# Weighted sums of two heads in one product, a selection cut into steps, and held-back loads in a four-layer decoder trunk

## The chip, the core and the metric

The kernel runs on one core of one Trainium2 chip. The core has five engines, each with an instruction stream of its own: TensorE (PE in the profile; its weight loads are shown apart as PEld), VectorE (DVE), ScalarE (ACT), GpSimd (POOL) and SyncE (SP). They wait for one another through semaphores. Transfers between HBM and on-chip memory go through queues that SP, ACT and GpSimd issue to, and share 16 DMA engines. TensorE reads its operands from SBUF and accumulates in PSUM.

The metric is the device time of one execution in microseconds. The kernel before took 2635.22 us, the median of three runs (2634.94 to 2639.01).

## The reference

Four decoder layers over one sequence of 256 positions, width 2048, all in float32. Layer i uses mixer i mod 3: latent attention (layers 0 and 3), sparse attention with a learned selection (layer 1), sliding-window attention (layer 2).

```
mem_n = rmsnorm(mem)
for each layer:
    h = rmsnorm(x)
    streams, mq, gate = split(h @ w_in)
    self_out = mixer(streams)                  # 2048 wide
    mem_out  = softmax(mq . mk / 16) . mv      # 4 heads of 256; mk, mv = mem_n @ w_mem_kv
    y = concat(self_out, mem_out) * silu(gate) # 3072 wide
    x = x + y @ w_out
out = rmsnorm(x)
```

- Latent: 16 heads; a query of 1536 compressed values gives each head 128 plain and 64 rotary values (`w_uq`); keys and values come from 512 compressed values (`w_ukv`); one rotary key serves all heads.
- Sparse: 32 heads of 64 in 4 groups; 16 small index heads score every key, and each query keeps its 64 best ones. A relative-position bias is added.
- Sliding window: 32 heads of 64 in 4 groups, window 128, a learned sink for each head, the same bias table.

## The kernel before

**Products in two parts.** Every weight is split into a high part rounded to fp32r and the remainder (`parts_of`, `split`, lines 60 and 64: ACT makes `wh`, DVE makes `wl`), and so are the activations. A product is then a sum of products of parts. Weights come in tiles `wr` (`stage`, line 197, on SP's queue, five buffers), each split and used once. `rows_by` (lines 227 to 229) puts positions on the output's partitions, with up to 512 weight columns as the moving side: six products for each block of 128 rows, three for each half of the positions. `columns_by` (lines 246 and 250) puts 128 weight columns on the partitions and moves 512 and 256 positions.

**Stages.** First the memory stage (`memory`): for all four layers, memory keys (`acc_mk`) and values (`acc_mv`) are computed and stored to HBM through GpSimd's queue, 2 MB for each of eight steps. In the same stage come the constants, the rows of x, and eight copies (`table_copies`, line 133, 1.5 MB each) that repeat the bias table for 128 partitions in HBM: two copies in step 1, none at the last step, one in each of the others. Then come the layers. Each layer begins with `first()`: keys and values of the mixer, for layer 1 also `select()`, for layers 1 and 2 also the padded values `vz` (two GpSimd fills and splits). Then six parts follow, in the order 4, 0, 1, 2, 3, 5, where 4 and 5 are the two halves of the memory attention and 0 to 3 the groups of self heads. Each part projects its queries and its gate (`acc_g`), attends, and gives `y`; the output projection of the part before (`w_out`, `acc_wo`, line 832 for the residual) is traced behind it.

**Order of work.** The order on each engine comes from a scheduler that works from a simulated timeline and the tile pools' buffers, so work traced behind other work may run ahead of it. `keep_in_program_order` pins an instruction behind all that was traced before it on its engine. GpSimd's queue is in order too: the memory keys and values are loaded on it (`mvr` line 480, `mkr` line 483), as are the bias blocks `bm` (line 775).

**Self attention of layers 1 and 2** (`Grouped.attend`). For each of eight heads of a group: scores (`sp`), softmax, transposes of the weights to PSUM (`ptp`, line 427), a split into `pT` and `hl` (128 x 384, the three blocks of 128 that the causal order leaves), and the weighted sum `o` (line 811): for key half 0 three products of 256 columns, for key half 1 three of 128. The heads go in the order 0 to 7. `vz` holds a group's 64 value columns with 64 zero columns ahead and behind, so that an even head lands on partitions 64 below its odd neighbour and both accumulate in the same rows of `o`. After four heads `gated` multiplies by the gate.

**Selection** (`Grouped.select`, lines 738 to 764). For each half of the queries: 16 heads of two products (`isp`), a ReLU on ACT, a running weighted sum on DVE, then eight rounds of "eight largest" and "replace them" on DVE (lines 760 and 761).

**Rotary queries of layers 0 and 3** (`Latent.project`, lines 610 to 619). For each of four groups the 64 rotary columns of four heads, 256 in all, go through `rows_by` (`acc_qr`, 12 blocks of 128 rows), then through `rope` on DVE, a split, four transposes (`tr`, from `qrs`) and a copy to `qrT`.

Of the kernel before, what the change touches and what calls it, by code (L numbers as in the profile page):

```python
# [8 lines left out]
F32 = mybir.dt.float32  # L9
# [18 lines left out]
PQ, AUX, WR = 5, 3, 5  # L28
# [3 lines left out]
def kernel(ctx: ExitStack, tc: tile.TileContext, a: dict, out: bass.AP,  # L32
# [23 lines left out]
    def part_tile(dt=F32R):  # L56
        return wk.tile([P, 512], dt, name="hl", tag="hl", bufs=3)
# [76 lines left out]


# [69 lines left out]

    def parts_of(wr, c0, n):
        wh = wp.tile([P, 512], F32R, name="wh", tag="wh", bufs=3)
        wl = wp.tile([P, 512], F32R, name="wl", tag="wl", bufs=3)
        split(wh[:, :n], wl[:, :n], wr[:, c0:c0 + n])
        return wh, wl  # L210

    def rows_by(xt, kts, w, k0, cols, name, prepare=None):


        acc = [ps.tile([P, 512], F32, name=f"acc_{name}{t}", tag="acc", bufs=4) for t in range(2)]
        for s in range(0, kts, ST):
            m = min(ST, kts - s)
            wr, n = stage(w, k0 + s, m, cols)
            if prepare is not None and s % 4 == 0:
                prepare(s // 4)  # L220
            for k in range(m):
                wh, wl = parts_of(wr, k * n, n)
                q = xt[(s + k) // 4]
                for t in range(2):
                    xh, xl = (q[:, v, (s + k) % 4, t * P:(t + 1) * P] for v in range(2))
                    first, last = s + k == 0, s + k == kts - 1
                    nc.tensor.matmul(acc[t][:, :n], xh, wh[:, :n], start=first, stop=False)  # L227
                    nc.tensor.matmul(acc[t][:, :n], xh, wl[:, :n], start=False, stop=False)  # L228
                    nc.tensor.matmul(acc[t][:, :n], xl, wh[:, :n], start=False, stop=last)  # L229
        return acc  # L230

    def columns_by(xt, kts, w, k0, cols, name):

        acc = [ps.tile([P, 2, S], F32, name=f"acc_{name}{j}", tag="acc", bufs=4) for j in range(2)]
        for s in range(0, kts, 2 * ST):
            m = min(2 * ST, kts - s)
            wr, n = stage(w, k0 + s, m, cols)
            for k2 in range(0, m, 2):
                wh, wl = parts_of(wr, k2 * S, 2 * S)
                for k in range(2):  # L240
                    kt = s + k2 + k
                    q = xt[kt // 4]

                    for j in range(2):
                        o = k * S + j * P
                        nc.tensor.matmul(acc[j], wh[:, o:o + P], q[:, :, kt % 4, :],  # L246
                                         start=kt == 0, stop=False)
# [57 lines left out]
    def memory():  # L305
# [50 lines left out]
        copies = [(v, g) for v in range(2) for g in range(4)]  # L356
        for i in range(depth):
            w = a["w_mem_kv"][i]
            for p_ in range(2):
# [116 lines left out]
    def memory_project(nm, i, w, mq0, g0, part):  # L476
        kT, qT = [], []
        v = [act.tile([P, 2, 512], F32R, name="mvr", tag="aux", bufs=AUX) for z in range(2)]
        for z in range(2):
            nc.gpsimd.dma_start(v[z], mv[i][part][:, z])  # L480
        for h in range(2):
            k = act.tile([P, 2, 2, S], F32R, name="mkr", tag="pq", bufs=PQ)
            nc.gpsimd.dma_start(k, mkT[i][2 * part + h])
# [7 lines left out]
    def memory_attend(nm, kT, v, qT, gT):  # L491
        y = act.tile([P, 2, 4, S], F32R, name="y", tag="y", bufs=2)
        for h in range(2):
# [21 lines left out]
            pH, pL = (wk.tile([P, 512], F32R, name="pT", tag="pT", bufs=2) for z in range(2))  # L515
# [23 lines left out]
    class Latent:  # L539
# [6 lines left out]
        def first(self):  # L546
# [11 lines left out]
            for t in range(2):  # L558
# [6 lines left out]
                hl = wk.tile([P, 2, 2, A_ROPE], F32R, name="krh", tag="krh", bufs=1)  # L565
# [38 lines left out]

        def project(self, g):
# [4 lines left out]
            qr = act.tile([P, 4, S], F32R, name="qrT", tag="aux", bufs=AUX)  # L610
            v = act.tile([P, 2, 512], F32, name="va", tag="aux", bufs=AUX)
            acc = rows_by(self.cT[:3], 12, wq, 0, (g * 768, 4, 192, A_NOPE, A_ROPE), "qr")
            for t in range(2):
                rr = wk.tile([P, 4, A_ROPE], F32, name="qrr", tag="z", bufs=3)
                rope(rr, acc[t][:, :S].rearrange("p (h d) -> p h d", h=4), t, 4)
                rs = wk.tile([P, 4, 2, A_ROPE], F32R, name="qrs", tag="qrs", bufs=1)
                split(rs[:, :, 0, :], rs[:, :, 1, :], rr)
                transposed(lambda i0, i1: qr[:, i0:i1, t * P:(t + 1) * P],
                           [rs[:, h].rearrange("p a b -> p (a b)") for h in range(4)])
# [13 lines left out]
            return qn, qr, kn, v, gate(self.nm, self.w, self.g0 + g * 512)  # L633

        def attend(self, qn, qr, kn, v, gT):
            y = act.tile([P, 2, 4, S], F32R, name="y", tag="y", bufs=2)
            for h in range(4):
# [15 lines left out]
                pT = wk.tile([P, 512], F32, name="pT", tag="pT", bufs=2)  # L653
# [10 lines left out]
    class Grouped:  # L664
# [7 lines left out]
        def first(self):  # L672
# [10 lines left out]
            if self.sparse:  # L683
                self.select()
# [34 lines left out]
        def select(self):  # L719
# [17 lines left out]
            nc.vector.tensor_scalar(iw, iw, 0.25, None, op0=OP.mult)  # L737
            for b in range(2):
# [3 lines left out]
                for h in range(16):  # L742
# [9 lines left out]
                    else:  # L752
                        nc.vector.scalar_tensor_tensor(sco[1 - cur][:, :n], rl[:, :n], c,
                                                       sco[cur][:, :n], op0=OP.mult, op1=OP.add)
                        cur = 1 - cur
                nc.vector.tensor_add(sco[1 - cur][:, :n], sco[cur][:, :n], caus[:, S - n:])
                cur = 1 - cur
                for it in range(8):
# [3 lines left out]
                    cur = 1 - cur  # L762
                nc.vector.tensor_scalar(self.sel[:, b, :n], sco[cur][:, :n], -2e38, NEG,
                                        op0=OP.is_gt, op1=OP.mult)

# [13 lines left out]
        def attend(self, g, q, bm, gT):  # L779
            y = act.tile([P, 2, 4, S], F32R, name="y", tag="y", bufs=2)  # L780
            for h in range(8):
# [24 lines left out]
                c0 = (h // 2 % 2) * S  # L806
                v0 = g * P + (64 if h % 2 == 0 else 0)
                for t in range(2):
                    ks = slice(t * S, t * S + S - t * P)
                    for n_, (z, p_) in enumerate(((0, pH), (0, pL), (1, pH))):  # L810
                        nc.tensor.matmul(o[:, c0 + t * P:c0 + S], self.vz[z][:, t, v0:v0 + P], p_[:, ks],
                                         start=h % 2 == t == n_ == 0, stop=h % 2 == t == 1 and n_ == 2)
                if h % 4 == 3:
                    gated(y, o, gT, (h // 4) * 2)
# [4 lines left out]
    memory()  # L819

    for i in range(depth):
# [23 lines left out]
        for n_, part in enumerate(order):  # L845
            if part >= 4:
                y = memory_attend(*memory_project(nm, i, mixer.w, mixer.mq0, mixer.g0, part - 4))
# [91 lines left out]
```

## Time and profile before

| | |
|---|---|
| median of three runs | 2635.22 us (2634.94 to 2639.01) |
| profiled execution | 2636.8 us |
| its span, first to last instruction | 2634.7 us |
| TensorE busy, products | 2601.2 us, 14556 |
| VectorE busy | 1884.1 us |
| ScalarE busy | 1628.8 us |
| GpSimd busy | 57.3 us |
| mean granted TensorE clock | 0.997 |
| moved by DMA | 511.70 MB, 194 GB/s |

How to read the rows. A group of instructions is named by line, engine, operation and "output<-inputs"; behind the shape stands the count, then the busy time in us, the mean duration of one in ns, and the idle time of the engine just before them. Products overlap one another, so the pace of TensorE is read from the distance of their starts and not from their durations. A row of the waits gives who waited for whom, the total in us, how often, and the longest. A row of the timeline gives start, length, and in brackets the idle time before. A row of windows gives for each engine the busy time, and behind them the granted clock, the share of the DMA engines and GB/s. "SPq" is an engine's own instruction queue.

### The profile page before, as it was taken

The numbers are of one execution on the slowest core, as the hardware profiler recorded it, in microseconds if no ns is written. First come the engines' busy times: TensorE is split into PE (matmuls) and PEld (weight loads), VectorE is DVE, ScalarE is ACT, GpSimd is POOL, SyncE is SP. The second block draws the span as 40 slices with busy tenths as digits, with TensorE's granted clock in tenths as the row PEclk, the third lists the DMA queues.
The fourth block names the chain that finished last, engine by engine and source line by source line (L and its number), as shares of the span: only waits on it lengthen the run. The fifth ranks groups of instructions, "written<-read, shape, count | busy, mean of one in ns | idle before, by whom it ended". The sixth has DMA issues, their size and how long they took to land.

```text
span 2634.7 us, 42943 instructions
## 1 busy us (share of the span) xinstructions
PE 2601.2 (99%) x14556; PEld 2254.7 (86%) x14556; DVE 1884.1 (72%) x4171; ACT 1628.8 (62%) x3476; POOL 57.3 (2%) x101
## 2 busy tenths in 40 slices
PE   8999999999999999999999999999999999999998
PEld 7888888888888889888888888888888888888886
DVE  6566656677767685877777776777778767776767
ACT  6455556556656566666666666676666655665655
POOL 1000000000000000000000000000000000000000
PEclk9999999999999999999999999999999999999999
DMA  9889886666557665555555555555555666655764
GB/s 305 279 287 300 281 256 198 166 185 168 169 160 224 192 192 172 167 183 170 173 163 191 188 190 177 173 172 178 189 168 162 205 165 186 165 170 156 226 183 135
DMA packets 456924, 511.70 MB, mean 194 GB/s; under 512 B 69584, under 2 KB 352480, under 8 KB 455552
## 3 DMA queue, kind: packets, MB, share of 16 engines
q1 hardware_dynamic: 443328, 451.75, 56.5%
q0 software_dynamic: 13088, 56.16, 6.6%
q8 instruction: 114, 1.87, 0.3%
q14 instruction: 106, 0.87, 0.1%
q10 hardware_dynamic: 288, 1.05, 0.1%
HBM read 489.91 MB, written 31.56 MB: 198 GB/s over the span
## 4 chain that ended last, share of the span: by engine, by line
PE 97%; DMA 1%; DVE 1%; ACT 0%; issue 0%; SPq 0%; ACTq 0%
PE acc_g L246 14%; PE acc_g L250 7%; PE acc_wo L227 7%; PE acc_wo L228 7%; PE acc_wo L229 7%; PE acc_mq L246 5%; PE acc_mk L246 5%; PE acc_qn L246 3%; PE acc_cq L246 3%; PE acc_mq L250 2%; PE acc_mk L250 2%; PE acc_q L227 2%; PE acc_q L228 2%; PE acc_q L229 2%; PE acc_mv L227 2%; PE acc_mv L228 2%
## 5 line engine op out<-in xcount | busy, mean ns | idle before, releaser
L64 DVE TENSOR_TENSOR wl<-wr,wh 128x512 fp32r<-128x512 f32 (+2 forms) x1776 | 1173.8, 664 | 645.1 <-ACT wh L60 614.2
L60 ACT ACTIVATE wh<-wr 128x512 fp32r<-128x512 f32 (+2 forms) x1776 | 1079.0, 609 | 837.3 <-PE acc_g L246 183.7
L246 PE MATMUL acc_g<-xT,wh 128*128 128x512 f32 x1536 | 489.0, 397 | 0.6 <-DVE z L257 0.6
L250 PEld LDWEIGHTS acc_g<-xT,wl 128*128 128x128 f32 x1536 | 285.2, 188 | 60.7
L250 PE MATMUL acc_g<-xT,wl 128*128 128x256 f32 x1536 | 311.0, 280 | 0.0
L228 PE MATMUL acc_wo<-wl,y 128*128 128x512 f32 x768 | 302.6, 394 | 0.6 <-DVE wl L64 0.5
L229 PE MATMUL acc_wo<-wh,y 128*128 128x512 f32 x768 | 299.1, 390 | 0.0
L246 PEld LDWEIGHTS acc_g<-xT,wh 128*128 128x128 f32 x1536 | 238.1, 189 | 4.8 <-issue 1.1
L227 PE MATMUL acc_wo<-wh,y 128*128 128x512 f32 x768 | 240.4, 393 | 0.7 <-ACT wh L60 0.6
L228 PEld LDWEIGHTS acc_wo<-wl,y 128*128 128x128 f32 x768 | 144.3, 188 | 30.0 <-DVE wl L64 1.4
L229 PEld LDWEIGHTS acc_wo<-wh,y 128*128 128x128 f32 x768 | 144.2, 188 | 28.4
L227 PEld LDWEIGHTS acc_wo<-wh,y 128*128 128x128 f32 x768 | 141.3, 188 | 27.8 <-ACT wh L60 1.0
L246 PE MATMUL acc_mk<-mT,wh 128*128 128x512 f32 x512 | 161.9, 398 | 2.4 <-ACT wh L60 2.4
L246 PE MATMUL acc_mq<-xT,wh 128*128 128x512 f32 x512 | 161.7, 397 | 0.0
L832 DVE TENSOR_TENSOR x<-x,acc_wo 128x512 f32<-128x512 f32 x192 | 125.7, 683 | 7.1 <-PE acc_wo L229 6.8
L246 PE MATMUL acc_qn<-cT,wh 128*128 128x512 f32 x384 | 123.2, 399 | 0.0
L246 PE MATMUL acc_cq<-xT,wh 128*128 128x512 f32 x384 | 120.8, 396 | 0.0
L250 PEld LDWEIGHTS acc_mk<-mT,wl 128*128 128x128 f32 x512 | 96.7, 189 | 23.4 <-DVE wl L64 0.8
L250 PEld LDWEIGHTS acc_mq<-xT,wl 128*128 128x128 f32 x512 | 93.7, 188 | 20.0
L250 PE MATMUL acc_mq<-xT,wl 128*128 128x256 f32 x512 | 102.5, 281 | 0.0
L228 PE MATMUL acc_q<-wl,xT 128*128 128x512 f32 x256 | 102.4, 400 | 0.0
L250 PE MATMUL acc_mk<-mT,wl 128*128 128x256 f32 x512 | 101.7, 280 | 0.0
(280 smaller groups left out, 4438.0 us busy)
## 6 DMA issues: line engine op xcount, KB each, us to landing
wr<-in_w_out_dram SPq DMA_DIRECT2D x192, 512.0 KB, 3.7
wr<-in_w_in_a_dram SPq DMA_DIRECT2D x176, 512.0 KB, 4.1
wr<-in_w_mem_kv_dram SPq DMA_DIRECT2D x128, 512.0 KB, 5.6
wr<-in_w_in_b_dram SPq DMA_DIRECT2D x112, 512.0 KB, 3.5
wr<-in_w_in_c_dram SPq DMA_DIRECT2D x104, 512.0 KB, 3.5
wr<-in_w_uq_dram SPq DMA_DIRECT2D x288, 128.0 KB, 2.6
tab<-flat POOLq DMA_DIRECT2D x8, 1536.0 KB, 11.1
wr<-in_w_in_a_dram SPq DMA_DIRECT2D x32, 288.0 KB, 3.0
```

What stands on the lines that cost most here:

```text
L60: nc.scalar.activation(o, i, AF.Copy, scale=scale)
L64: nc.vector.tensor_sub(lo, src, f32(hi))
L227: nc.tensor.matmul(acc[t][:, :n], xh, wh[:, :n], start=first, stop=False)
L228: nc.tensor.matmul(acc[t][:, :n], xh, wl[:, :n], start=False, stop=False)
L229: nc.tensor.matmul(acc[t][:, :n], xl, wh[:, :n], start=False, stop=last)
L246: nc.tensor.matmul(acc[j], wh[:, o:o + P], q[:, :, kt % 4, :], start=kt == 0, stop=False)
L250: nc.tensor.matmul(acc[j][:, 0, :], wl[:, o:o + P], q[:, 0, kt % 4, :], start=False, stop=kt == kts - 1)
L832: nc.vector.tensor_add(xs, xs, acc[t])
```

## The change

Five edits.

1. *Rotary product for two groups.* `rotary(g)` runs in groups 0 and 2 alone, behind the values of the group: one `rows_by` over the eight heads of two groups (512 columns), then the rope for two groups and two halves of positions. The "aux" pool has 4 buffers instead of 3.
2. *Two heads' weighted sums in one product.* The heads go in the order 0, 2, 1, 3, 4, 6, 5, 7. Two heads that share the value columns (0 and 2, 1 and 3) put their split weights side by side in tiles of 3 x 2 x 128, and one product moves 512 columns for key half 0 and 256 for key half 1. The output `o` is thus ordered half of positions, pair, position; the product with the gate reads it in that order. The "pT" pool has 4 buffers of 768 instead of 2 of 512, "hl" 2 instead of 3.
3. *Selection step by step.* The loops of `select` become a generator, `selection`, which stops after each index head and after each round; `rows_by` and `columns_by` trace two steps of it for each weight tile, and the first `attend` of layer 1 traces what is left. The padded values follow the selection.
4. *Table copies held back.* The eight copies leave the memory stage. Each is traced behind the first quarter of an output projection: six in layer 0, two in layer 1. `not_before(col)` puts a GpSimd copy of one column of the new residual ahead of it, pinned, so that the transfer waits for it.
5. *First memory keys held back.* In part 4 of each layer a `not_before` on the mixer's key tile stands ahead of the loads of the values and keys, which are pinned too.

Beside these, the scratch space for the descriptors of GpSimd's transfers is set to 8192 bytes for each partition, and the small rotary-key tile shares a buffer with `qrs`.

```diff
-PQ, AUX, WR = 5, 3, 5
+PQ, AUX, WR, PT = 5, 4, 5, 4
...
+    def not_before(col):
+        tc.keep_in_program_order(nc.gpsimd.tensor_copy(small("tick", 1), col))
...
+    steps = []
+    def other_work():
+        for _ in range(2):
+            if steps and next(steps[0], None) is None:
+                steps.pop()
...
             wr, n = stage(w, k0 + s, m, cols)
+            other_work()
...
-                for c in copies[:2 if step == 1 else 1]:
-                    table_copies(*c)
-                copies = copies[2 if step == 1 else 1:]
...
-    def memory_project(nm, i, w, mq0, g0, part):
+    def memory_project(nm, i, w, mq0, g0, part, behind):
         kT, qT = [], []
+        if part == 0:
+            not_before(behind)
...
+        pin = tc.keep_in_program_order if part == 0 else lambda inst: inst
         for z in range(2):
-            nc.gpsimd.dma_start(v[z], mv[i][part][:, z])
+            pin(nc.gpsimd.dma_start(v[z], mv[i][part][:, z]))
...
+        def rotary(self, g):
+            self.qr = [act.tile([P, 4, S], F32R, name="qrT", tag="aux", bufs=AUX) for z in range(2)]
+            acc = rows_by(self.cT[:3], 12, a["w_uq"][self.j], 0, (g * 768, 8, 192, A_NOPE, A_ROPE), "qr")
+            for t in range(2):
+                for z in range(2):
+                    rr = wk.tile([P, 4, A_ROPE], F32, name="qrr", tag="z", bufs=3)
+                    rope(rr, acc[t][:, z * S:(z + 1) * S].rearrange("p (h d) -> p h d", h=4), t, 4)
+                    rs = wk.tile([P, 4, 2, A_ROPE], F32R, name="qrs", tag="qrs", bufs=1)
+                    split(rs[:, :, 0, :], rs[:, :, 1, :], rr)
+                    transposed(lambda i0, i1: self.qr[z][:, i0:i1, t * P:(t + 1) * P],
+                               [rs[:, h].rearrange("p a b -> p (a b)") for h in range(4)])
...
-            return qn, qr, kn, v, gate(self.nm, self.w, self.g0 + g * 512)
+            if g % 2 == 0:
+                self.rotary(g)
+            return qn, self.qr[g % 2], kn, v, gate(self.nm, self.w, self.g0 + g * 512)
...
             if self.sparse:
-                self.select()
+                steps.append(self.select())
+            else:
+                self.spaced_values()
...
         def attend(self, g, q, bm, gT):
+            while steps:
+                other_work()
...
-            for h in range(8):
+            for h in (0, 2, 1, 3, 4, 6, 5, 7):
...
-                pH, pL = wk.tile([P, 512], F32R, name="pT", tag="pT", bufs=2), part_tile()
-                split(pH[:, :3 * P], pL[:, :3 * P], tp[:, :3 * P])
-                if h % 4 == 0:
+                half, odd = h // 2 % 2, h % 2
+                if half == 0:
+                    pHL = [wk.tile([P, 3, 2, P], F32R, name="pT2", tag="pT", bufs=PT) for z in range(2)]
+                split(pHL[0][:, :, half, :], pHL[1][:, :, half, :],
+                      tp[:, :3 * P].rearrange("p (i c) -> p i c", i=3))
+                if half == 0:
+                    continue
+                if not odd:
                     o = misc("o")
...
                 for t in range(2):
-                    ks = slice(t * S, t * S + S - t * P)
-                    for n_, (z, p_) in enumerate(((0, pH), (0, pL), (1, pH))):
-                        nc.tensor.matmul(o[:, c0 + t * P:c0 + S], self.vz[z][:, t, v0:v0 + P], p_[:, ks],
-                                         start=h % 2 == t == n_ == 0, stop=h % 2 == t == 1 and n_ == 2)
+                    for n_, (z, p_) in enumerate(((0, 0), (0, 1), (1, 0))):
+                        nc.tensor.matmul(o[:, t * S:], self.vz[z][:, t, v0:v0 + P],
+                                         pHL[p_][:, 2 * t:2 + t].rearrange("p i h c -> p (i h c)"),
+                                         start=odd == t == n_ == 0, stop=odd == t == 1 and n_ == 2)
...
+                if c == 0 and copies:
+                    not_before(xs[:, :1])
+                    table_copies(*copies.pop(0))
...
-    nc = _bacc.Bacc("TRN2", target_bir_lowering=False, num_devices=1)
+    nc = _bacc.Bacc("TRN2", target_bir_lowering=False, num_devices=1,
+                     dynamic_dma_scratch_size=8192)
```

More of the change, by code (lines that the diff above doesn't have):

```diff
@@ L514, in memory_attend @@
             tp = weights_T(es, [(0, 0), (1, 0), (0, 1), (1, 1)])
[L515 removed]
+            pH, pL = (wk.tile([P, 768], F32R, name="pT", tag="pT", bufs=PT)[:, :512] for z in range(2))
             split(pH, pL, tp)
@@ L564, in first @@
                 rope(kr, raw[:, None, :A_ROPE], t, 1)
-                hl = wk.tile([P, 2, 2, A_ROPE], F32R, name="krh", tag="krh", bufs=1)
+                hl = wk.tile([P, 4, 2, A_ROPE], F32R, name="krh", tag="qrs", bufs=1)[:, :2]
                 for d in range(2):
@@ L737, in select, with selection @@
             nc.vector.tensor_scalar(iw, iw, 0.25, None, op0=OP.mult)
+            return self.selection(iqT, ikd, iw)
+        def selection(self, iqT, ikd, iw):
             for b in range(2):
@@ L819 @@
     memory()
+    copies = [(v, g) for v in range(2) for g in range(4)]
     for i in range(depth):
@@ L846 @@
             if part >= 4:
-                y = memory_attend(*memory_project(nm, i, mixer.w, mixer.mq0, mixer.g0, part - 4))
+                y = memory_attend(*memory_project(nm, i, mixer.w, mixer.mq0, mixer.g0, part - 4,
+                                                  f32(mixer.k[:, 0] if kind else mixer.kr)[:, 0, :1]))
             else:
```

33 lines of the change are left out of this document (16 added, 17 removed).

## The prediction

> **What bounds the kernel.** I read the page first, then who waited for whom on TensorE, then the timeline of TensorE in steady stretches and around its gaps, then GpSimd's timeline at those gaps. The page:
>
> ```profile
> span 2634.7 us, 42943 instructions
> ...
> PE 2601.2 (99%) x14556; PEld 2254.7 (86%) x14556; DVE 1884.1 (72%) x4171; ACT 1628.8 (62%) x3476; POOL 57.3 (2%) x101
> ...
> GB/s 305 279 287 300 281 256 198 166 185 168 169 160 224 192 192 172 167 183 170 173 163 191 188 190 177 173 172 178 189 168 162 205 165 186 165 170 156 226 183 135
> ...
> PE 97%; DMA 1%; DVE 1%; ACT 0%; issue 0%; SPq 0%; ACTq 0%
> ```
>
> TensorE is busy 99% of the span and is 97% of the chain that ended last. Two things alone can move the time: fewer or denser products, and the few gaps. The first six slices (0 to 395 us, the memory stage) move 256 to 305 GB/s, the later ones mostly 160 to 190. The gaps, from the waits of TensorE:
>
> ```profile
> PE acc_mv L227 <- ACT wh L60: 10.0, 2, 8.7
> PE acc_kvb L227 <- ACT wh L60: 3.1, 1, 3.1
> PE acc_mk L246 <- ACT wh L60: 2.4, 1, 2.4
> PE o L811 <- ACT pT L60: 1.7, 3, 0.6
> PE ptp L427 <- ACT e L60: 1.4, 3, 0.5
> ```
>
> The 8.7 us is the start, which the change leaves alone. So 1.3 + 3.1 + 2.4 = 6.8 us are waits for weight parts and 1.7 + 1.4 = 3.1 us waits around the weighted sums of layers 1 and 2.
>
> **Rotary product for two groups.** It replaces 576 products of 256 columns (3 x 192) by 288 of 512: the order of the changed program has 192 + 96 of these. The columns stay the same, so only what a product costs beside its columns can be saved. The pace, first and last row of a steady run of each width:
>
> ```profile
> L228 PE MATMUL acc_qr<-wl,cT 128*128 128x256 f32 x192 | 52.0, 290 | 0.0
> L229 PE MATMUL acc_qr<-wh,cT 128*128 128x256 f32 x192 | 50.6, 283 | 0.0
> L227 PE MATMUL acc_qr<-wh,cT 128*128 128x256 f32 x192 | 40.3, 286 | 0.0
> ...
> 519.56 0.40 PE L227 MATMUL acc_qr<-wh,cT 128*128 128x256 f32 x2
> 525.31 0.40 PE L227 MATMUL acc_qr<-wh,cT 128*128 128x256 f32 x2
> ...
> 2608.04 0.62 PE L227 MATMUL acc_wo<-wh,y 128*128 128x512 f32 x2
> 2609.40 1.07 PE L227 MATMUL acc_wo<-wh,y 128*128 128x512 f32 x4
> ```
>
> From 519.56 to 525.31 start 48 products (eight blocks of six): 0.120 us each. From 2608.04 to 2609.40 start six: 0.227 us each. Saved: 576 x 0.120 - 288 x 0.227 = 69.1 - 65.4 = 3.7 us, all on the path. The durations of 283 to 290 ns are no pace, since products overlap.
>
> [...]
>
> The weight loads shrink from 96 transfers of 128 KB to 48 of 256 KB on SP's queue, and 96 pairs of half-width weight splits become 48 full ones on ACT and DVE. Both engines are at 62% and 72%, so that is worth nothing. The rope and the transposes keep their count but move into the gate product, where ACT and DVE run the same kind of load; the transposes stand there with 22 to 24 products between them, as they did among acc_qn, where TensorE shows no wait for them. Zero; at worst 0.5 us for each of 16, the size of the waits above, 8 us.
>
> **Two heads' sums in one product.** 384 products (192 of 256 columns, 192 of 128) become 96 of 512 and 96 of 256. One head now:
>
> ```profile
> L811 PE MATMUL o<-pT,vz 128*128 128x256 f32 x128 | 35.3, 284 | 1.7 <-ACT pT L60 1.7
> L811 PE MATMUL o<-pT,vz 128*128 128x128 f32 x128 | 28.5, 248 | 0.0
> ...
> 1196.09 0.28 PE L811 MATMUL o<-pT,vz 128*128 128x256 f32 x1
> ...
> 1196.61 0.28 PE L811 MATMUL o<-pT,vz 128*128 128x128 f32 x1
> 1196.72 0.68 PE L227 MATMUL acc_q<-wh,xT 128*128 128x512 f32 x2
> 1197.24 0.40 PE L228 MATMUL acc_q<-wl,xT 128*128 128x512 f32 x1
> ```
>
> Six products take 1196.09 to 1196.72 = 0.63 us, and the two wide ones behind them 0.52 instead of 2 x 0.227: 0.065 us more, lost behind the 128-column product. 64 heads x 0.695 = 44.5 us. After: 32 pairs x (3 x 0.227 + 3 x 0.120) = 33.3 us, with no 128-column product left in it. Saved: 11.2 us. [...]
>
> The waits around the sums (3.1 us): each stood where weights' transposes, sums and scores of neighbouring heads met with no weight product between. In the order of the changed program none of the sums follows such a transpose directly. I take all 3 us as gone; between 0 and 3.1. Next late is the softmax chain of two heads instead of one, with 10 to 40 weight products as cover; without it a wait is 0.6 us again. The four other buffers (PT, AUX, hl, big) cost no instruction; hl falls from 3 to 2 but loses its 64 uses in the sums. I put 1 us against it.
>
> **Copies and first keys held back.** GpSimd's queue ahead of the three gaps, then TensorE:
>
> ```profile
> 107.69 1.06 POOL L133 DMA_DIRECT2D tab<-flat  x2
> ...
> 289.66 0.53 POOL L133 DMA_DIRECT2D tab<-flat  x1
> ...
> 379.88 1.08 POOL L480 DMA_DIRECT2D mvr<-mv  x2
> 380.93 0.56 POOL L483 DMA_DIRECT2D mkr<-mkT  x1
> ...
> L133 POOL DMA_DIRECT2D tab<-flat x8: 529/530/547, 52.3 to 336.0; - x8
> ...
> wr<-in_w_mem_kv_dram SPq DMA_DIRECT2D x128, 512.0 KB, 5.6
> ```
>
> ```profile
> 126.38 0.73 PE L246 MATMUL acc_mk<-mT,wh 128*128 128x512 f32 x2 [2.44 <-ACT wh L60]
> ...
> 131.06 0.62 PE L246 MATMUL acc_mk<-mT,wh 128*128 128x512 f32 x2
> ...
> 131.76 0.63 PE L246 MATMUL acc_mk<-mT,wh 128*128 128x512 f32 x2
> ...
> 293.57 0.73 PE L227 MATMUL acc_mv<-wh,mT 128*128 128x512 f32 x2 [1.26 <-ACT wh L60]
> ...
> 391.92 0.53 PE L227 MATMUL acc_kvb<-wh,xT 128*128 128x288 f32 x2 [3.11 <-ACT wh L60]
> ...
> 396.96 0.43 PE L227 MATMUL acc_kvb<-wh,xT 128*128 128x288 f32 x2
> ...
> 397.75 0.42 PE L227 MATMUL acc_kvb<-wh,xT 128*128 128x288 f32 x2
> ```
>
> Behind the gap at 126.38 a step of two wide and two narrow products takes (131.06 - 126.38) / 4 = 1.17 us instead of 0.70, so 1.9 us are lost beside the 2.4. Behind that at 391.92 it is (396.96 - 391.92) / 4 = 1.26 instead of 0.79: 1.9 beside 3.1. The three waits with both tails are 6.8 + 3.8 = 10.6 us. I take 9 as gone, since the stores of memory keys and values stay in the stage; bounds 0 and 10.6.
>
> What it costs: 12 one-column copies on GpSimd (2% busy), and behind each of them the queue. Behind a residual column wait one table copy, later a bias load or a key load of part 5, none due for some 20 us; behind the key column wait four loads of 512 KB, wanted after two acc_mq products (128 x 2 products, over 40 us). The copies now run beside the output projection, at 160 to 190 GB/s instead of 280. Six of the eight ran singly in the busier stage, and only the one at 289.66 stands near a wait (1.3 us at 293.57). I take 1 us for all; at worst each stalls like the double one, 8 x 4.3 = 34 us.
>
> **Selection step by step.** The counts stay: 64 products, the sums, 16 rounds of maximum and replacement.
>
> ```profile
> L760 DVE MAX8 m<-sco 128x8 f32<-128x256 f32 x8 | 3.4, 422 | 0.0
> L761 DVE MATCH_REPLACE8 sco<-m,sco 128x256 f32<-128x256 f32 x8 | 3.3, 410 | 0.0
> ...
> 1040.00:1090.00 50.00, 50.00 (x323) 46.10 (x321) 35.20 (x87) 31.96 (x76) 1.06 (x1) 1.00 0.61 183
> 1090.00:1140.00 50.00, 50.00 (x284) 43.50 (x283) 45.05 (x112) 31.96 (x71) 2.12 (x3) 1.00 0.53 165
> ```
>
> TensorE (second number) has no gap there now, so nothing can be gained. The new order puts the last score products later, with about 120 gate products and 56 of the output projection before the first weights' transpose, over 30 us of cover for 8 x 0.83 = 6.7 us on a DVE at 45 of 50 us. If DVE falls behind, up to 6.7 us of it shows. I take 1 us.
>
> **Sum.** -3.7 - 11.2 - 3 - 9 + 1 + 1 + 1 = -23.9 us. The profiled execution took 2636.8 us (span 2634.7), so 2612.9; the median of the runs is 1.6 us lower, 2611.3.
>
> **Rivals.**
> 1. The weight waits stay, because the stage's own loads and stores make them: for it, the weights alone are 512 KB for every twelve products of 0.227 us, 192 of the stage's 280 GB/s, and stores of keys and values come on top; against it, a copy or key load stands 4 to 19 us ahead of each. Without the 9 us: 2620.
> 2. The products cost by their columns alone, 0.227 us for each 512, and what looks like a price of the narrow ones is spent again behind the wide ones: both parts save nothing, 2611.3 + 14.9 = 2626. The rows 0.120 and 0.227 speak against it. [...]
> 3. The held-back copies starve the output projection's weights, in layers 0 and 1 (slower). At 4.3 us each: 2611.3 + 34 - 1 = 2645. It decides from (23.9 + 1) / 8 = 3.1 us for each copy. The double copy did cost that; single copies in a busier stage did not.
> 4. The change does not do what it says: the waits only move, to the pair of heads (3 us), the transposes among the gates (8 us), the late selection (6.7 us) and one copy (4.3 us): 2611.3 + 22 = 2633.
>
> **Numbers.** Forecast 0.64, rival 1 0.18, rival 2 0.06, rival 3 0.06, rival 4 0.06. A change under 0.2% (5.3 us) is about what a measurement of this kernel can't tell from none. Faster 0.64 + 0.18 + 0.06 = 0.88, same 0.06, slower 0.06. Low end: 14.9 + 10.6 + 3.1 saved, nothing lost, and 0.065 us at some 100 further changes from one kind of product to another that fall away where sums are merged: 35 us, 2600, and 1 us for rounding. High end: rival 2, 2626. Rivals 3 and 4 and the tails of the others stay outside.
>
> **What would show it.** acc_qr with 288 products of 512 columns 0.227 us apart; o with 96 of 512 and 96 of 256, none of 128; TensorE's busy time down by some 15 us; no wait of acc_mk, acc_kvb above 1 us, and the first six slices near 230 GB/s. Wrong if TensorE waits for wh at acc_wo in layers 0 and 1, for e or pT at ptp and o, for qrs at tr, or if six sums take over 1.1 us.

## The result and the profile after

The changed kernel takes 2607.73 us, the median of four runs (2605.6 to 2610.79), against 2636.04 us of the kernel before in the same session (2634.94 to 2639.01). The ratio is 0.9893, with a 95% interval of 0.9878 to 0.9908: 28 us faster, between 24 and 32. The forecast was 2611. The profiled execution took 2605.6 us, its span is 2603.8 us.

The page of the changed kernel: span, busy times of the engines, GB/s in forty slices.

```profile
span 2603.8 us, 41703 instructions
...
PE 2579.8 (99%) x14076; PEld 2220.4 (85%) x14076; DVE 1875.0 (72%) x4123; ACT 1617.9 (62%) x3428; POOL 61.9 (2%) x113
...
GB/s 289 248 259 252 256 211 235 186 170 190 191 204 217 198 214 215 168 195 182 200 166 196 171 220 170 177 170 186 194 156 150 234 182 169 170 167 182 211 178 129
```

TensorE is busy 21.4 us less (2601.2 to 2579.8) where the prediction looked for "some 15", and the span is 30.9 us shorter. So about 9.5 us came from gaps. Some 3.8 us of the busy time aren't fewer products either: they are the two stretches at a lower clock behind the waits of acc_mk and acc_kvb (granted clock 0.59 and 0.57), which are gone too (the last section shows them). Here is what is left of the gaps, in the waits of TensorE (who waited for whom, total, times, longest):

```profile
PE acc_mv L240 <- ACT wh L60: 9.4, 4, 8.5
PE o L847 <- DVE pT L64: 0.3, 1, 0.3
```

Beside the start (8.5 us) there remain 1.2 us. The waits of acc_kvb and acc_mk are gone, and with them that of `ptp`; of `o` 0.3 us is left. Where the span became shorter can be read from acc_cq, the first product behind the mixer's keys in layers 0 and 3. Its first and last start, before and after:

```profile
L246 PE MATMUL acc_cq<-xT,wh x384: 387/395/475, 404.9 to 2118.3; 128*128 128x512 f32 x192
```

```profile
L260 PE MATMUL acc_cq<-xT,wh x384: 387/395/478, 394.3 to 2088.2; 128*128 128x512 f32 x192
```

The memory stage with the first keys is 10.6 us shorter in these two profiles, the stretch from there to the last acc_cq of layer 3 (1713.4 to 1693.9 us) 19.5, and the rest 0.8. The two merged products, in the groups by shape (`acc_qr` has two more groups of 96 like the one shown):

```profile
L242 PE MATMUL acc_qr<-wh,cT 128*128 128x512 f32 x96 | 37.4, 389 | 0.0
...
L847 PE MATMUL o<-pT,vz 128*128 128x512 f32 x96 | 32.6, 400 | 0.3 <-DVE pT L64 0.3
...
L847 PE MATMUL o<-pT,vz 128*128 128x256 f32 x96 | 16.7, 282 | 0.0
```

Their pace, from the timeline of TensorE (start, length):

```profile
542.02 0.62 PE L240 MATMUL acc_qr<-wh,cT 128*128 128x512 f32 x2
543.38 0.62 PE L240 MATMUL acc_qr<-wh,cT 128*128 128x512 f32 x2
...
1189.51 1.23 PE L847 MATMUL o<-pT,vz 128*128 128x512 f32 x6
1190.58 0.64 PE L240 MATMUL acc_q<-wh,xT 128*128 128x512 f32 x2
```

Six rotary products take 1.36 us, 0.227 each. The six of a pair of heads take 1.07 us, where 3 x 0.227 + 3 x 0.120 = 1.04 were forecast.

### The profile page after: what moved, and what is told of

Same layout as the page of the kernel before. It is cut to its first block, busy times and chain, and to the rows that moved or that the text cites. A ratio compares the mean times of both kernels' runs of the same rounds, so it can differ in the third digit from the quotient of the medians.

```text
span 2603.8 us, 41703 instructions
## 1 busy us (share of the span) xinstructions
PE 2579.8 (99%) x14076; PEld 2220.4 (85%) x14076; DVE 1875.0 (72%) x4123; ACT 1617.9 (62%) x3428; POOL 61.9 (2%) x113
## 4 chain that ended last, share of the span: by engine, by line
PE 98%; DMA 1%; DVE 1%; ACT 0%; issue 0%; SPq 0%; ACTq 0%
PE acc_g L260 14%; PE acc_g L264 7%; PE acc_wo L240 7%; PE acc_wo L241 7%; PE acc_wo L242 7%; PE acc_mq L260 5%; PE acc_mk L260 4%; PE acc_cq L260 3%; PE acc_qn L260 3%; PE acc_mq L264 2%; PE acc_q L241 2%; PE acc_q L240 2%; PE acc_q L242 2%; PE acc_mk L264 2%; PE acc_mv L240 2%; PE acc_mv L241 2%
## 5 line engine op out<-in xcount | busy, mean ns | idle before, releaser
L241 PEld LDWEIGHTS acc_wo<-wl,y 128*128 128x128 f32 x768 | 144.3, 188 | 28.3 <-DVE wl L64 0.6
```

## The experiments

Twelve kernels ran in three sessions. The kernel before had a median of 2633.84, 2636.92 and 2635.78 us in them, and every ratio is against the runs of its own session. Differences are told as differences of these ratios, times 2636 us.

| kernel | median us | ratio to before (95%) |
|---|---|---|
| before + rotary pair | 2631.65 | 0.9993 (0.9984 to 1.0003) |
| before + paired sums | 2617.2 | 0.9938 (0.9923 to 0.9952) |
| before + copies held back | 2632.2 | 0.9995 (0.9985 to 1.0004) |
| before + keys held back | 2647.17 | 1.0052 (1.0037 to 1.0067) |
| before + selection in steps | 2637.63 | 1.0004 (0.9995 to 1.0014) |
| before + keys + selection in steps | 2632.9 | 0.9986 (0.9976 to 0.9996) |
| changed, selection in one piece | 2624.73 | 0.9955 (0.9940 to 0.9969) |
| changed, keys not held back | 2613.13 | 0.9911 (0.9896 to 0.9925) |
| changed, copies not held back | 2611.46 | 0.9905 (0.9890 to 0.9919) |
| changed, each copy twice at once | 2627.62 | 0.9965 (0.9953 to 0.9977) |
| changed, each copy twice, apart | 2607.6 | 0.9893 (0.9878 to 0.9907) |
| changed, two loads earlier | 2604.14 | 0.9881 (0.9866 to 0.9895) |

### The rotary product alone

```diff
-            acc = rows_by(self.cT[:3], 12, wq, 0, (g * 768, 4, 192, A_NOPE, A_ROPE), "qr")
+            if g % 2 == 0:
+                self.rotary(g)     # (g * 768, 8, 192, A_NOPE, A_ROPE)
```

> The kernel before with the rotary product for two groups alone (aux 4, the smaller scratch space). Theory (a product has a price beside its columns): 288 products of acc_qr at 0.227 us instead of 576 at 0.120, so -3.7 us, and no wait for qrs among the gate products. Rival 2 (columns alone): 0 us. A rival from the order of work (the rope and its transposes come late among the gates): up to +8 us. The three weight waits of the memory stage and of acc_kvb stay as before under all of them, 6.8 us of waits in all.

Measured 0.9993: 1.8 us, between 4.2 gained and 0.8 lost. The time alone doesn't tell it from nothing. Its page shows TensorE busy 4.0 us less, and no wait for `qrs` appeared:

```profile
PE 2597.2 (99%) x14268; PEld 2239.3 (85%) x14268; DVE 1876.8 (71%) x4123; ACT 1625.2 (62%) x3428; POOL 57.3 (2%) x101
```

By the starts of acc_cq in that trace (404.9 to 2116.4 us, span 2631.6) the stretch with layer 0 is 1.9 us shorter and the one with the rest of layer 3 1.2, together 3.1.

### The paired sums alone

```diff
-            for h in range(8):
+            for h in (0, 2, 1, 3, 4, 6, 5, 7):
...
-                        nc.tensor.matmul(o[:, c0 + t * P:c0 + S], self.vz[z][:, t, v0:v0 + P], p_[:, ks],
+                        nc.tensor.matmul(o[:, t * S:], self.vz[z][:, t, v0:v0 + P],
+                                         pHL[p_][:, 2 * t:2 + t].rearrange("p i h c -> p (i h c)"),
```

> The kernel before with the two heads' sums in one product alone (head order, pT 4, hl 2, the smaller scratch space). Theory: -11.2 us from the products and the loss behind the 128-column ones, and -3 to -4 from the six waits around the sums, together about -15 us. Rival 2 (columns alone): -3 to -4 us, from the waits only. A rival in which the waits only move to the pair: -11 us, with waits of o and ptp of 3 us still there.

Measured 0.9938: 16 us, between 13 and 20, more than half of the whole change. Rival 2 (columns alone count) falls. TensorE's busy time from its page, and the waits of layers 1 and 2 that it still has:

```profile
PE 2585.2 (99%) x14364; PEld 2236.8 (86%) x14364; DVE 1882.3 (72%) x4171; ACT 1622.4 (62%) x3476; POOL 57.4 (2%) x101
```

```profile
PE o L814 <- DVE pT L64: 0.3, 1, 0.3
PE acc_wo L228 <- DVE wl L64: 0.2, 1, 0.2
```

Busy time fell by 16.0 us, where the forecast had 11.2. Beside the waits of `o` and `ptp`, three small ones in layers 1 and 2 shrank with them that the forecast had not counted. These are they, in the waits of the kernel before between 1200 and 2000 us:

```profile
PE acc_g L246 <- DVE z L257: 0.6, 3, 0.2
PE acc_wo L227 <- ACT wh L60: 0.6, 1, 0.6
PE acc_wo L228 <- DVE wl L64: 0.5, 1, 0.5
```

With the 1.7 and 1.4 us of `o` and `ptp` that is 4.8 us, of which 0.5 is left, so 4.3 us of waits went. Not all of the 16.0 belongs to the sums, though. Of the 20.5 us by which the profiled span fell, 2.2 lie ahead of acc_cq, in the memory stage, which this edit doesn't touch:

```profile
L246 PE MATMUL acc_cq<-xT,wh x384: 387/395/476, 402.7 to 2097.8; 128*128 128x512 f32 x192
```

There the wait of acc_mk was 1.4 us instead of 2.4 in this execution. The waits ahead of acc_cq add up to 15.5 us in both kernels, so the 2.2 us were busy time; that they are the stretch at a lower clock behind acc_mk (1.9 us in the kernel before) is an estimate. The stretch from acc_cq to the last acc_cq fell by 18.3 us (1713.4 to 1695.1): that is the sums' part, 4.3 us of waits and about 14 of busy time.

### The copies alone, the keys alone

Two kernels. The first takes the copies out of the memory stage and puts each behind a quarter of an output projection:

```diff
+                if c == 0 and copies:
+                    not_before(xs[:, :1])
+                    table_copies(*copies.pop(0))
```

> The kernel before with the eight table copies held back alone. Theory (the copies made the waits of the memory stage): the 2.4 us wait of acc_mk and its slow tail go, and part of the 1.3 us wait of acc_mv; -4.5 to -5.5 us; the wait of acc_kvb (3.1 us) stays, since the first keys are not held back. Rival 1 (the stage's own loads and stores make them): 0 us. Rival 3 (the copies starve the output projection): waits of acc_wo for wh appear, up to +34 us.

The second holds back the first memory keys and values:

```diff
+        if part == 0:
+            not_before(behind)
...
-            nc.gpsimd.dma_start(v[z], mv[i][part][:, z])
+            pin(nc.gpsimd.dma_start(v[z], mv[i][part][:, z]))
```

> The kernel before with the first memory values and keys of each layer held back alone. Theory: the 3.1 us wait of acc_kvb and its 1.9 us tail go, -5.0 us, and no new wait at acc_cq, where the four loads then run; the wait of acc_mk (2.4 us) stays. Rival 1 (the narrow blocks of 288 columns make the wait themselves): 0 us, the wait stays. Rival (the loads hit the next product instead): the wait moves to acc_kvb or acc_cq, between -3 and 0 us.

The copies gave 0.9995, which is not told from nothing and misses the 4.5 us or more of the theory; the keys made the kernel slower, 1.0052, by 13.7 us. No theory had that. The waits of TensorE in the two kernels, the copies' first:

```profile
PE acc_kvb L232 <- ACT wh L60: 2.2, 1, 2.2
...
PE acc_mk L251 <- ACT wh L60: 0.5, 1, 0.5
```

```profile
PE isp L753 <- ACT rl L756: 5.6, 1, 5.6
PE acc_g L251 <- DVE mqT L271: 3.5, 1, 3.5
PE acc_mk L251 <- ACT wh L60: 2.1, 1, 2.1
```

Each part removes its own wait: the copies that of acc_mk (2.4 to 0.5 us), the keys that of acc_kvb (3.1 to none). But in the second kernel two new waits stand far from the one it removes, in and behind the selection of layer 1, whose lines weren't edited. Its timeline there (bracket: idle before, and who ended it):

```profile
1077.05 2.25 PE L753 MATMUL isp<-ikd,iqT 128*128 128x256 f32 x16
...
1078.68 0.30 DVE L768 MAX8 m<-sco 128x8 f32<-128x128 f32 x1
...
1083.70 0.23 DVE L771 TENSOR_SCALAR vs<-sco 128x128 f32<-128x128 f32 x1
1084.04 0.35 DVE L759 TENSOR_SCALAR sco<-rl,iw 128x256 f32<-128x256 f32 x1
1084.42 0.39 ACT L756 ACTIVATE rl<-isp 128x256 f32<-128x256 f32 x1 [3.18 <-DVE sco L759]
...
1084.86 4.98 PE L753 MATMUL isp<-ikd,iqT 128*128 128x256 f32 x16 [5.56 <-ACT rl L756]
```

DVE runs the rounds of the first half of the queries one straight after another, up to 1083.70. Only then does it read the scores of the second half, ACT gets its buffer back, and TensorE, which had no other work placed here, goes on after 5.56 us. Sixteen products then take 4.98 us instead of the 2.25 at 1077.05. By the sum: 5.6 + 3.5 of waits and 2.7 of slow products, most of what was lost.

### Keys with the selection in steps, and the steps alone

The index products (`isp`) of that kernel lie within 27 us (1062.5 to 1089.4); in the kernel before the scheduler had spread them over 38, and in the changed kernel the steps spread them over 67. In each row: duration in ns, first and last start in us. First before, then after, then the kernel with the keys alone:

```profile
L745 PE MATMUL isp<-ikd,iqT x64: 274/282/283, 1066.5 to 1104.7; 128*128 128x256 f32 x64
```

```profile
L772 PE MATMUL isp<-ikd,iqT x64: 274/283/287, 1057.8 to 1124.5; 128*128 128x256 f32 x64
```

```profile
L753 PE MATMUL isp<-ikd,iqT x64: 277/283/582, 1062.5 to 1089.4; 128*128 128x256 f32 x64
```

So the suspicion was that holding the loads back led the scheduler to another order, and that writing the selection as steps among the weight tiles makes its order independent of that. Two kernels test it; the first is the kernel before with both parts, the second the changed kernel without the steps.

```diff
             wr, n = stage(w, k0 + s, m, cols)
+            other_work()
...
-                self.select()
+                steps.append(self.select())
```

> The kernel before with two parts of the change: the first memory keys and values held back, and the selection step by step. Against the kernel before, whose runs lie near 2634 to 2636 us. Theory: holding the keys back alone cost 13.3 us because the planner, once the loads of the keys are pinned, put all the index products of layer 1 (isp) close together, so that PE waited 5.6 us for them and 3.5 us behind them and then ran at half clock; written as steps among the weight blocks they keep apart whatever the loads do. Then the waits of 5.6 and 3.5 us near 1085 to 1093 us are gone, the wait of acc_kvb (3.4 us) is gone too, and the time is 3 to 6 us below the kernel before (ratio near 0.998). Rival: what failed was room, the third buffer of the ring that the held-back values share, or the place of the held-back loads in POOL's queue, neither of which this kernel mends: about 13 us above the kernel before (ratio near 1.005).

```diff
-                steps.append(self.select())
-            else:
-                self.spaced_values()
+                self.select()
+            self.spaced_values()
...
-                    yield True
```

> The changed kernel with the selection of layer 1 written as one piece, as it stood before, everything else changed. Theory: the selection's products bunch again, PE waits for isp some 5 us and runs at half clock behind that: 10 to 15 us above the changed kernel's 2608, so 2618 to 2623 us. Rival (room or queue was at fault, which the changed kernel's fourth buffer mends): as the changed kernel, 2607 to 2609 us. The prediction, which priced the selection's steps at plus 1 us and no gain, would have it at 2606 to 2608 us.

Measured 0.9986 for the first: 3.7 us faster where the keys alone were 13 us slower, and the waits of `isp` and of acc_g for `mqT` are gone. The second has 0.9955, 16 us above the changed kernel, a little more than the 10 to 15 expected, and the waits are there again (its rows of the waits):

```profile
PE isp L767 <- ACT rl L770: 6.2, 1, 6.2
PE acc_g L260 <- DVE mqT L280: 3.5, 1, 3.5
```

The second kernel has the fourth buffer of "aux", so room wasn't the fault. The other half of the rival, the place of the held-back loads in GpSimd's queue, is not ruled out: the expectation says that the first of these kernels doesn't mend it, but it does. GpSimd's timeline in layer 1 of the kernel before, of the kernel with the keys alone, and of the changed kernel:

```profile
954.55 1.06 POOL L480 DMA_DIRECT2D mvr<-mv  x2 [61.66 <-PE mo L523]
```

```profile
1089.96 1.06 POOL L697 MEMSET vz<- 128x1152 f32 x1 [9.47 <-PE isp L753]
...
1091.09 1.06 POOL L488 DMA_DIRECT2D mvr<-mv  x2
```

```profile
995.53 1.09 POOL L493 DMA_DIRECT2D mvr<-mv  x2 [0.32 <-PE acc_iq L242]
...
1090.75 1.06 POOL L712 MEMSET vz<- 128x1152 f32 x1 [92.54 <-PE isp L772]
```

The padded values `vz` take the buffers of the index queries, so their fills on GpSimd wait for the index products. Where the selection is one piece, the fills are traced ahead of part 4, and a pinned load waits for all that was traced before it on its engine: the loads of the keys go out at 1091.09 us, behind the fills (at 1088.69 in the changed kernel without the steps). Where the padded values are traced with the end of the selection, the loads are free of them: 995.53, and 1002.06 in the kernel with keys and steps. So the held-back loads, which the first part of layer 1 needs, hung on the whole of the index products. The steps by themselves, on the kernel before:

> The kernel before with the selection step by step and nothing else, against the kernel before at 2634 to 2637 us. Theory: in the kernel before the planner keeps the index products apart already, so the steps alone gain and cost nothing: within 2 us. The prediction's step has plus 1 us. Rival, that the steps themselves are what gains in the changed kernel: 3 us or more below the kernel before.

Measured 1.0004: nothing. So the edit of the selection is worth nothing where the scheduler spreads the products anyway, and 16 us where it doesn't. The edit does two things: it cuts the selection into steps, and with the end of the selection it moves the fills behind the loads. No run has one without the other. That the scheduler bunches the products because the loads stand behind the fills is therefore read from the traces and the code, and not shown by a run.

### Without the keys held back, without the copies held back

Each is the changed kernel with one of the two parts undone: no `not_before` and no pins in `memory_project`, or the copies back in the memory stage.

> The changed kernel with the first memory keys and values of each layer not held back, everything else changed. Theory: with the copies alone held back the wait of acc_kvb was still 2.2 us, so it is back here with 2 to 3.4 us and a stretch of half clock behind it: 3 to 6 us above the changed kernel's 2608, so 2611 to 2614 us. Rival: with the copies gone from the memory phase the loads of the keys collide with nothing: 2607 to 2609 us, no wait of acc_kvb above 1 us.

> The changed kernel with the table copies back in the memory phase, two in its step 1 and one in each of steps 2 to 7, everything else changed. Theory: the waits of acc_mk (2.4 and 1.3 us before) come back with a stretch of half clock: 4 to 6 us above 2608, so 2612 to 2614 us. Rival, by the run of the copies held back alone (1.6 us, not told from nothing): 2607 to 2610 us. Had the copies' new place a price that hides a gain, the time would be below 2607 us.

Measured 0.9911 (4.7 us above the changed kernel) and 0.9905 (3.2 us above). The intervals of both overlap that of the changed kernel, so it is their waits that tell. Without the keys held back:

```profile
PE acc_mv L240 <- ACT wh L60: 11.2, 4, 8.8
PE acc_kvb L240 <- ACT wh L60: 2.8, 1, 2.8
```

Without the copies held back:

```profile
PE acc_mv L240 <- ACT wh L60: 9.6, 3, 8.2
PE acc_mk L260 <- ACT wh L60: 3.8, 2, 2.1
```

Each wait comes back with its own cause, and only with it. The traces of all fourteen kernels agree: acc_mk waits 1.4 to 3.8 us in the seven with the copies in the memory stage and at most 0.5 in the seven without; acc_kvb waits 2.2 to 4.7 us in the six that don't hold the keys back and not at all in the eight that do. The stretch of half clock that the first expectation has behind acc_kvb didn't come (the clock was 1.00 there, by the rows of the last section); the wait of 1.3 us that the second one gives to acc_mk was one of acc_mv. The small waits of acc_mv come and go (0 to 4.9 us beside the first) whatever a kernel does, and with them the memory stage differs by up to 5.7 us between profiles of kernels that are alike there.

### What the copies cost where they are now

Two kernels issue each held-back copy a second time. The first does it at the same moment:

```diff
+        tc.keep_in_program_order(nc.gpsimd.dma_start(spare[v][g].rearrange("p h n -> p (h n)"), src))
```

> The changed kernel with each of the eight held-back table copies issued twice, the second into a table of its own that nothing reads: twice the traffic of the copies in the output projections where they now lie. Theory: they are covered there, at most plus 1 us: 2607 to 2609 us, and no wait of acc_wo above 1 us. Rival (the copies starve the weight loads of the output projection): each further copy costs up to 4.2 us, 2608 plus up to 34 us, with waits of acc_wo for their weights at the eight places.

The second does it two blocks of the projection later:

```diff
+                if c == 2 and again:
+                    not_before(xs[:, :1])
+                    spare_copies(*again.pop())
```

> The changed kernel with a second copy of each held-back table, as in the run with each copy issued twice (2627.6 us), but issued two blocks of the output projection later (c = 2, some 11 us) rather than at the same moment. Theory: what starves the weights is two copies in a row, 15 us of landing against the stages that are loaded ahead; a copy alone fits, so apart they cost little: 2608 to 2612 us. Rival: the stretch has no room for the bytes at all, whenever they come: 2622 to 2630 us as in that run.

At once: 0.9965, 19 us above the changed kernel, where the theory allowed 1; 2.4 for each further copy on average, in the profile 1.8 for each of the six in layer 0 and 4.0 for each of the two in layer 1. Apart: 0.9893, nothing. The same bytes in the same projections thus cost 19 us or none. The waits of TensorE in the first kernel between 580 and 1300 us (the second has none there):

```profile
PE acc_q L243 <- ACT wh L60: 3.4, 2, 1.9
PE acc_qn L263 <- ACT wh L60: 2.9, 3, 1.2
PE acc_mq L263 <- ACT wh L60: 2.8, 1, 2.8
PE acc_kv L243 <- ACT wh L60: 1.8, 1, 1.8
```

Not the projection starves, as the rival had it (acc_wo is not in the list), but the product that follows it, whose weights are loaded while the copies run: of two copies issued at 596.44 and 596.97 us the second runs until 612 to 614, and ahead of 613.65 acc_qn waits 1.02 us for its weights. Over that whole profile ACT waits 14.8 us, three times, for loads of `w_in_b` to land. In the first kernel a copy lands 9.1 to 11.2 us after its issue, the second behind it after 15.1 to 17.1. In the second kernel the two are issued 11 to 15 us apart and land after 8.3 to 10.9 us each, so one has landed before the next starts. And a single copy costs nothing where it is now: from the first product of acc_wo to its last in layer 0 the profile has 383.4 us in the changed kernel and in the one without the copies there.

### Two loads earlier

```diff
-                weighted_parts(q, features(a["l_x"], c), 64 + c * 4)
+                weighted_parts(q, xft.pop(0), 64 + c * 4)     # loaded one memory step earlier
...
+        if not begun:
+            begun.append(True)
+            for k in range(m):
+                nc.sync.dma_start(dst[:, k, :], src[:, k, cols[0]:cols[0] + n])
```

> The changed kernel with two loads put differently: the features of x (l_x) issued one memory step before the step that uses them, and the very first weight load in two halves. Theory: the three waits of acc_mv that the changed kernel still has beside the first (0.9 us together) go, and the first product starts 1 to 2 us before the 8.5 us at which it starts now: 2605 to 2607 us. Rival: the features held a step longer take buffers of the ring that the memory keys use, and the memory phase waits for them: 2608 to 2612 us.

Measured 0.9881, 3.2 us below the changed kernel, but the intervals overlap and its profiled span (2604.9 us) isn't shorter than the changed kernel's (2603.8). Its first wait is 8.0 us instead of 8.5, but that wait lies between 7.9 and 9.1 over all fourteen traces; of the 0.9 us of acc_mv 0.4 is left, and acc_mk waits 0.5. Whether it is faster than the changed kernel stays open.

## Why the prediction was right, and where it was not

**Rotary product: right by the rows.** Forecast 3.7 us; the pace is 0.227 us as used, TensorE's busy time fell by 4.0, layers 0 and 3 became 3.1 us shorter, and the time fell by 1.8 (between -0.8 and 4.2).

**Two heads' sums: right mechanism, too small.** Forecast 11.2 + 3 us, less 1 for other effects; measured 16 us (13 to 20), in the profile of layers 1 and 2 about 14 of busy time and 4.3 of waits. The pair's own price was right (1.07 us against 1.04). What was mis-sized is the side of the kernel before: 0.695 us for each head came from one head whose six products stood together. Added up over the traces, from each start to the next and without the waits, the sums took 42.4 us before and 34.4 paired, 8.0 less where the forecast's terms give 7.0. The loss behind them was about as forecast: 59 changes from a 128-column sum to a weight product, on average 0.064 us late, are 3.8 us against 64 x 0.065 = 4.2, and behind a 256-column sum there is next to none (0.006). The other 2 us of busy time could not be traced to rows; that stays open. Of the waits, 1.7 us of acc_g and acc_wo had been overlooked.

**Copies and first keys: right in sum, as two causes.** Forecast 9 of 10.6 us; undoing one part or the other costs 3.2 and 4.7, together 7.9, each with its own wait. The profiles agree: acc_cq starts at 402.7 to 407.8 us in the four kernels that hold back neither (mean 405.1) and at 394.3 to 400.0 in the five that hold back both (mean 396.8), 8.3 us apart, so the 10.6 us between the two profiles above are partly luck. Rival 1 (the stage's own loads make the waits) falls. The copies' price of 1 us was nothing: one copy at a place is free, a second at once costs 2.4 us on average. So rival 3's mechanism exists. Even with two copies at once it stays, on average, under the 3.1 us for each copy from which it would have decided; in layer 1 alone it passes them (4.0).

The first six slices were to show "near 230 GB/s" and show 289 to 211, 253 over the first 395 us against 285. The missing 32 GB/s x 395 us = 12.6 MB are eight copies of 1.5 MB: a copy's bytes are counted once in these rows. Counted twice, as read and as written, they would have given 221, close to the forecast, which doesn't say how it came to its figure.

**Selection: the step that failed.** The prediction said that TensorE has no gap there, "so nothing can be gained", and put +1 us for lateness. Neither the gap nor the gain can be seen in the trace of before, because both come with another part of the change: with the keys' loads held back, the scheduler bunches the index products, and without the edit of the selection the change is 16 us dearer. That the sum came out is in this respect luck: the edit cancels a loss that the forecast didn't know of. Priced part by part on the kernel before, the parts give 1.8 + 16.3 + 1.3 for rotary, sums and copies, a loss of 13.7 for the keys and 1 for the steps, 4.7 us in all; what was measured is 28.

**Rivals.** Rivals 2 and 4 fall with the paired sums (16 us) and with the waits that are gone. Rival 3 falls with the copies at no cost. The forecast of 23.9 us less is 28.3 by the medians. By the profiles, one for each kernel and so good to a few us, the paired sums gave 18.3 where 13.2 were forecast (11.2 + 3 - 1), the weight waits 8.3 where it was 8 (9 - 1), the rotary part 3.1 where it was 3.7, and what the selection cost is at most 0.7 (18.3 + 1.9 - 19.5) where it was 1. So the term that was mis-sized is that of the sums.

## What to carry to other kernels

Where a scheduler sets the order of the work, a part that is tried alone may be slower and still be half of a gain: look where the new wait stands, and whether an edit has touched that place at all. Ahead of pinning an instruction, look at what is traced before it on its engine: here two fills that waited for the whole selection. Where an order must hold (rounds of DVE between weight splits), it can be written into the program instead of being left to a planner that happens to find it. And in this kernel a held-back transfer of 1.5 MB was free (383.4 us for acc_wo in layer 0 with it and without), two at once were not (19 us for eight pairs), and two issued 11 to 15 us apart were (0.9893 both with and without the second).

## What the runs showed of the hardware

In the kernel before, two short waits cost TensorE more than their length. These are windows of TensorE in the kernel before, ahead of, behind and well behind the waits of 2.44 and 3.11 us (stretch, its length, busy time with count, granted clock, DMA share, GB/s):

```profile
120.00:123.50 3.50, 3.50 (x17) 1.00 0.82 200
126.40:130.20 3.80, 3.80 (x12) 0.59 1.06 341
131.00:134.00 3.00, 3.00 (x19) 1.00 1.08 340
...
392.80:396.40 3.60, 3.60 (x19) 0.57 0.63 169
397.00:400.00 3.00, 3.00 (x25) 1.00 0.62 171
```

Over the 3.8 and 3.6 us behind the waits the granted clock is 0.59 and 0.57 on average. The sixteen products from 126.38 to 131.06 us take 4.68 us, where the next steps of four take 0.70 each, 2.8 for sixteen: behind the wait of 2.44 us 1.9 us more are lost. The length of the wait alone doesn't decide it. In the changed kernel without the keys held back the clock stays at 1.00 behind the wait of acc_kvb of 2.79 us; in the one without the copies held back it is at half behind a wait of acc_mk of 1.64 us:

```profile
388.70:392.50 3.80, 3.76 (x26) 1.00 0.64 166
```

```profile
278.20:281.40 3.20, 3.20 (x12) 0.50 0.52 143
```

What decides it these runs don't show. With the longer waits of the keys held back alone (5.56 us up to 1084.86, then 3.48 up to 1093.31) it is 0.79 over the last 5 us of the first wait and half from there on, through the products behind it and the second wait (windows of that kernel):

```profile
1080.00:1085.00 5.00, 0.14 (x1) 0.79 0.02 6
1085.00:1090.00 5.00, 4.84 (x16) 0.50 0.00 0
1090.00:1095.00 5.00, 1.69 (x5) 0.50 0.51 142
```

In the rows of the kernel before the clock is at 1.00 again from 131.00 and 397.00 us on, 4.6 and 5.1 us behind the first product after the wait. The fall came here after 2.44 and 1.64 us, and not after 2.79.
